# Adding expert rows into the residual by accumulating transfers instead of loads and vector additions

## The chip, the cores and the metric

The kernel runs on one core of a Trainium2 chip. The core has five engines with an instruction queue each: PE (matrix products), DVE (vector), ACT (scalar), POOL (GpSimd) and SP (sync, which here only issues transfers), and 16 DMA engines that all queues share. The metric is the device time of one execution in microseconds. Before the change the median of three runs is 1189.38 us (1186.39 to 1190.62).

## The reference

One transformer block on x of shape [1, 512, 1024], all in fp32: three attention-like branches, a merge, a first residual with layer norm, then a hierarchical mixture of experts (the router picks one of 4 groups and 2 of 8 experts in it, so each of 512 tokens goes to 2 of 32 experts), a second residual and a layer norm. Only the end concerns this change:

```python
    y = jnp.zeros((T, D), h.dtype).at[tok_s].add(w_s[:, None].astype(h.dtype) * ybuf[dest])
...
        y = _hier_moe(x, w_router_group[l], b_router_group[l], w_router_expert[l], b_router_expert[l], w_exp_gate[l], w_exp_up[l], w_exp_down[l])
        x = _layer_norm(DN_ALPHA * x + y, ln2_g[l], ln2_b[l])
```

A token's output is DN_ALPHA (2 to the power 1/4) times its row of x, plus the weighted rows of its two experts, normalized.

## The kernel before, in words

The first 880 us compute the branches, the merge, the first layer norm and the router. The residual x1 stays in SBUF as four chunks c of 128 tokens by 1024. A copy of it goes to DRAM (x1d), from which tokens are gathered for the experts.

The experts' stage walks over 16 pairs of experts, p = 0 to 15. Each pair has 64 rows for either expert. Its 12 weight tiles of 512 KB (tiles j = 0 to 3 gate and up, j = 4 and 5 down) come from DRAM through SP's queue into a ring of 33 buffers (`expert_raw`, load at L114), 96 MB in all. Per pair: `gather` brings the rows (for pairs 0 and 1 by one-hot products with x1 on PE, L767; later by an indirect transfer and transposes, L778), `gate_up` makes 16 matmuls (L789), ACT and DVE make the gated product `esg` (L193, L194, L1006), PE transposes it (L1010), ACT copies it to `ehT` (L1011), and 8 matmuls with the down weights give the rows (L1023). The profile shows each fp32 matmul of these as two records.

What becomes of the rows depends on the pair. For pairs 0 to 13 (PDR = 14) ACT and DVE scale them and POOL scatters them into the DRAM buffer yd (L1037): row k * 512 + t is the k-th expert's row of token t. After the scatter of pair 13 the program reads yd back in eight loads of 512 KB on SP's queue (L1046, into buffers of the ring) and adds them to x1 on DVE (L1048 for k = 0, with the factor ALPHA; L1050 for k = 1). Pairs 14 and 15 do not pass through DRAM: their rows `yp` stay in SBUF as a high and a low part (L1033, L1034), and one-hot products `ohs` put them in place (`add_up`, L982).

The end: for chunk c and half n an accumulator in PSUM gets the matmul identity times x1 (L1062), two one-hot products with pair 14's rows, two with pair 15's; the layer norm reads it (L631 and on) and SP stores the result.

The order of instructions on each engine is chosen by a scheduler when the program is built, from dependences and its own costs; every engine then takes its own instructions strictly in that order, and an instruction that waits holds up all that stand behind it on its engine. The waits on transfers are by semaphores: DMAHW for those of SP, DMASW for those of POOL, eight of each in turn.

Of the kernel before, what the change touches and what calls it, by code (L numbers as in the profile page):

```python
# [16 lines left out]
OP = mybir.AluOpType  # L17
# [5 lines left out]
ALPHA = 2.0 ** 0.25  # L23
# [13 lines left out]
def build(tc, ins, out, dbg=None):  # L37
    nc = tc.nc
# [4 lines left out]
    def T(pool, shape, dt=F32, tag=None, **kw):  # L43
        cnt[0] += 1
        tag = tag or f"u{cnt[0]}"
        return pool.tile(list(shape), dt, name=f"{tag}_{cnt[0]}", tag=tag, **kw)

    def dump(name, ap):
        if name in dbg:
            nc.sync.dma_start(dbg[name], ap)  # L50
# [19 lines left out]
    V, S, TE, G = nc.vector, nc.scalar, nc.tensor, nc.gpsimd  # L70
# [4 lines left out]
    def bank(tag, w=512, dt=F32):  # L75
        t = T(ps, [128, 512], dt, tag=tag)
        return t[:, :w] if w != 512 else t
# [10 lines left out]
    yd = T(mdram, [1024, 1024], tag="yd")  # L88
# [102 lines left out]
    def silu2(t, src):  # L191

        S.activation(t, src, AF.Tanh, scale=0.5)  # L193
        V.scalar_tensor_tensor(t, t, 1.0, src, op0=OP.add, op1=OP.mult)  # L194
# [73 lines left out]
    with cpool:  # L268
        for h in range(4):
# [13 lines left out]
            for c in range(4):  # L283
# [6 lines left out]
                p = T(tp, [128, 256], tag="cp")  # L290
# [262 lines left out]
    x1 = T(sp, [128, 4, 1024], tag="x1")  # L553
# [49 lines left out]
    for k in range(8):  # L603
        S.mul(mh[:, k, :], merged[:, k, :], 0.5)
        V.scalar_tensor_tensor(ml[:, k, :], merged[:, k, :], 0.5, mh[:, k, :].bitcast(F32),
                               op0=OP.mult, op1=OP.subtract)
    p1a.close()

    rp = es.enter_context(tc.tile_pool(name="rawb", bufs=NRAW))
# [5 lines left out]
    def expert_raw(n):  # L615

        while len(raws) < min(n, 192):
            m = len(raws)
            e, j = m // 12 * 2 + m % 2, m % 12 // 2
            pool, tag = ring[m % len(ring)]  # L620
            raws[e, j] = load(ins["wexp"][e, j], pool=pool, tag=tag)
# [100 lines left out]
    for k in range(8):  # L722
        raw = wo_raw[k]
        w0 = T(wp, [128, 1024], F32R, tag="wh", bufs=3)
        split(w0[:, :512], w0[:, 512:], raw[:, :512])
        t = T(wp, [128, 1024], F32R, tag="wl", bufs=3) if k < 3 else T(rp, [128, 1024], F32R, tag="raw")
# [23 lines left out]
    def fetch(p):  # L750
        if PEG <= p < 16:
            G.indirect_dma_start(out=xgs[p % AHEAD], out_offset=None, in_=x1d[:, :],
                                 in_offset=bass.IndirectOffsetOnAxis(ap=gidx[:, p:p + 1], axis=0),
                                 bounds_check=511, oob_is_err=False)

    def gather(p):

        xs = T(mp, [128, 8, 128], tag="xs")
        pts = []
        if p < PEG:  # L760
            oh_ = oh0 if p == 0 else T(mp, [128, 4, 128], tag="ohg", bufs=1)
            pts = [bank("o" if p == 0 else "tr") for _ in range(2)]
            for c in range(4):
                if p > 0:
                    picked(c, p, oh_)
                for k in range(8):
                    TE.matmul(pts[k // 4][:, k % 4 * 128:(k % 4 + 1) * 128], x1[:, c, k * 128:(k + 1) * 128],  # L767
                              oh_[:, c, :], start=c == 0 and k % 4 == 0, stop=c == 3 and k % 4 == 3)
        else:
            xg = xgs[p % AHEAD]  # L770
        for j in range(2):
            if p < PEG:
                pt = pts[j]
            else:
                pt = bank("tr")
                for k in range(4):
                    kk = j * 4 + k
                    TE.transpose(pt[:, k * 128:(k + 1) * 128], xg[:, kk * 128:(kk + 1) * 128], ident)  # L778
            (S.copy if j == 0 else V.tensor_copy)(xs[:, j * 4:(j + 1) * 4, :].rearrange("p k r -> p (k r)"), pt)
        return xs  # L780

    def gate_up(p, xs):

        acc = bank("pj")
        for j in range(4):
            for k in range(2):
                for q in range(2):
                    rows_ = slice(q * 64, (q + 1) * 64)
                    TE.matmul(acc[rows_, :], xs[:, j * 2 + k, rows_], raws[2 * p + q, j][:, k * 512:(k + 1) * 512],  # L789
                              start=j == 0 and k == 0, stop=j == 3 and k == 1)  # L790
        return acc
# [200 lines left out]
    for p in range(16):  # L992
        expert_raw(12 * p + 12 + len(ring))
        gu = gate_up(p, xs)
        if p == 0:
            part = Parts(T(mp, [128, 2048], tag="yp"))
            tables(part)
            overflow_tables(part)
            for j in range(1, AHEAD + 1):
                fetch(j)  # L1000
        if p < 15:
            xs = gather(p + 1)
            fetch(p + 1 + AHEAD)
        sg = T(mp, [128, 256], tag="esg")
        silu2(sg, gu[:, :256])
        V.tensor_tensor(sg, sg, gu[:, 256:], op=OP.mult)  # L1006
        hT = T(mp, [128, 256], tag="ehT")
        pt = bank("tr", 256)
        for k in range(2):
            TE.transpose(pt[:, k * 128:(k + 1) * 128], sg[:, k * 128:(k + 1) * 128], ident)  # L1010
        S.mul(hT, pt, 0.5)  # L1011
        if p < PDR:
            y = T(mp, [128, 2048], tag="yp")
        else:
            yp = T(mp, [128, 2, 1024], F32R, tag="yp")
            ohs = T(mp, [128, 512], F32R, tag="ohs")
            V.tensor_scalar(ohs, i512, tok[:, p:p + 1], None, op0=OP.is_equal)
        for n in range(2):
            acc = bank("o")
            for k in range(2):  # L1020
                for q in range(2):
                    rows_ = slice(q * 64, (q + 1) * 64)
                    TE.matmul(acc[rows_, :], hT[:, k * 128 + q * 64:k * 128 + (q + 1) * 64],  # L1023
                              raws[2 * p + q, 4 + k][:, n * 512:(n + 1) * 512],
                              start=k == 0, stop=k == 1)
            ns = slice(n * 512, (n + 1) * 512)
            if p < PDR:
                if n == 0:
                    S.mul(y[:, ns], acc, wsl[:, p:p + 1])
                else:  # L1030
                    V.tensor_scalar(y[:, ns], acc, wsl[:, p:p + 1], None, op0=OP.mult)  # L1031
            else:
                S.mul(yp[:, 0, ns], acc, wsl[:, p:p + 1])  # L1033
                V.scalar_tensor_tensor(yp[:, 1, ns], acc, wsl[:, p:p + 1], yp[:, 0, ns].bitcast(F32),  # L1034
                                       op0=OP.mult, op1=OP.subtract)
        if p < PDR:
            G.indirect_dma_start(out=yd[:, :], out_offset=bass.IndirectOffsetOnAxis(ap=yidx[:, p:p + 1], axis=0),  # L1037
                                 in_=y[:, 0:1024], in_offset=None, bounds_check=1023, oob_is_err=False)
        else:
            group.append((ohs, yp))  # L1040
        if p == PDR - 1:

            for c in range(4):
                for k in range(2):
                    t = T(rp, [128, 1024], tag="raw")
                    nc.sync.dma_start(t, yd[k * 512 + c * 128:k * 512 + (c + 1) * 128, :])  # L1046
                    if k == 0:
                        V.scalar_tensor_tensor(x1[:, c, :], x1[:, c, :], ALPHA, t, op0=OP.mult, op1=OP.add)  # L1048
                    else:
                        V.tensor_tensor(x1[:, c, :], x1[:, c, :], t, op=OP.add)  # L1050
    dump("gidx", gidx)


# [140 lines left out]
```

## Time and profile before

| | |
|---|---|
| median of three runs | 1189.38 us |
| profiled execution, its own time | 1191.01 us |
| its span, first to last instruction | 1189.1 us |
| mean granted TensorE clock | 0.985 |
| PE, DVE, ACT, POOL busy | 93%, 42%, 37%, 7% |
| SP's transfers (q1) | 183.92 MB, 45.6% of 16 engines' span |
| POOL's transfers (q0) | 15.87 MB, 4.1% |

The shares are means over stages with different limits. From about 950 us to 1145 us the 16 DMA engines are full and PE waits for weights between matmuls; before that PE is nearly always busy. The chain of waits follows what ended last back from the end; a matmul's place in it gives its line. A time of a transfer "to landing" runs from its issue to its semaphore.

### The profile page before, as it was taken

Reading aid. Unit: us, or ns where it says so; the run is one execution under the profiler, and the core shown is the slowest. Engines: PE = TensorE matmul, PEld = TensorE weight load, DVE = VectorE, ACT = ScalarE, POOL = GpSimd, SP = SyncE. Lnnn points to the kernel's source line nnn. Section 1 sums busy time; section 2 is a strip of 40 time slices with the busy share of each in tenths; the row PEclk is TensorE's granted clock in tenths of the full one; section 3 lists DMA queues with packets and bytes.
Section 4 is the critical chain, followed back from the end, with each engine's and each line's share of the span. In section 5 each row is a group of like instructions: output and inputs, shape, how many; then the busy total and the mean of one; then the engine's idle time right before and its main releaser. Section 6 shows DMA issues by size and latency. Waiting matters only on the chain.

```text
span 1189.1 us, 17191 instructions
## 1 busy us (share of the span) xinstructions
PE 1111.0 (93%) x6830; PEld 779.2 (66%) x6830; DVE 504.1 (42%) x998; ACT 442.9 (37%) x762; POOL 84.7 (7%) x104
## 2 busy tenths in 40 slices
PE   6999999999999999999999999999989988888872
PEld 4788677777777887887887877888774333223231
DVE  4544387776676323323224223336574111111145
ACT  6965467665655433233233333225011111101112
POOL 1000130000000000000000000000323111110003
PEclk9999999999999999999999999999999999999986
DMA  8633241222222632322331333335659999999961
GB/s 295 217 94 88 91 130 54 64 81 64 80 63 80 185 105 62 93 89 66 98 97 49 93 91 130 121 100 214 262 195 240 314 408 405 402 403 399 410 254 71
DMA packets 69650, 200.91 MB, mean 169 GB/s; under 512 B 16719, under 2 KB 18843, under 8 KB 69568
## 3 DMA queue, kind: packets, MB, share of 16 engines
q1 hardware_dynamic: 62640, 183.92, 45.6%
q0 software_dynamic: 6928, 15.87, 4.1%
q8 instruction: 55, 0.90, 0.3%
q14 instruction: 27, 0.22, 0.1%
HBM read 191.23 MB, written 17.81 MB: 176 GB/s over the span
## 4 chain that ended last, share of the span: by engine, by line
PE 76%; DMA 13%; ACT 4%; DVE 3%; issue 2%; SPq 0%; ACTq 0%; POOL 0%; DVEq 0%; POOLq 0%
PE pj L131 49%; DMA raw<-in_wexp_dram 11%; PE pj L789 5%; PE tr L217 3%; PE o L1023 3%; PE pj L718 2%; PE o L718 2%; DMA raw<-in_w_in_dram 1%; PE sc L357 1%; PE sc L511 1%; DMA wh<-in_wexp_dram 1%; PE o L533 1%; ACT bvt L338 1%; PE o L299 1%; PE o L530 1%
## 5 line engine op out<-in xcount | busy, mean ns | idle before, releaser
L84 DVE TENSOR_TENSOR wl<-raw,wh 128x1024 fp32r<-128x1024 f32 (+1 forms) x129 | 148.1, 1149 | 268.3 <-PE pj L131 179.1
L83 ACT CAST wh<-raw 128x1024 fp32r<-128x1024 f32 (+1 forms) x137 | 132.3, 967 | 247.9 <-PE pj L131 237.5
L131 PE MATMUL pj<-xh,wh 128*128 128x512 f32 x760 | 204.5, 401 | 5.1 <-ACT wh L83 5.1
L131 PE MATMUL pj<-xl,wh 128*128 128x512 f32 x760 | 199.8, 397 | 0.0
L131 PE MATMUL pj<-xh,wl 128*128 128x512 f32 x760 | 194.1, 394 | 0.0
L131 PEld LDWEIGHTS pj<-xh,wl 128*128 128x128 f32 x760 | 141.8, 188 | 32.5 <-issue 2.1
L131 PEld LDWEIGHTS pj<-xh,wh 128*128 128x128 f32 x760 | 139.8, 189 | 35.1 <-ACT wh L83 6.4
L131 PEld LDWEIGHTS pj<-xl,wh 128*128 128x128 f32 x760 | 140.7, 188 | 29.7 <-issue 0.9
L789 PE MATMUL pj<-raw,xs 128*64 128x512 f32 x432 | 125.2, 605 | 13.0 <-DMA raw<-in_wexp_dram 12.1
L789 PEld LDWEIGHTS pj<-raw,xs 128*64 128x64 f32 x432 | 36.0, 137 | 82.3 <-issue 49.3
L193 ACT ACTIVATE esg<-pj 128x256 f32<-128x256 f32 x16 | 6.1, 384 | 134.8 <-PE pj L789 134.8
L194 DVE SCALAR_TENSOR_TENSOR esg<-esg,pj 128x256 f32<-128x256 f32 x16 | 6.7, 421 | 116.8 <-ACT esg L193 116.8
L1023 PE MATMUL o<-raw,ehT 128*64 128x512 f32 x204 | 52.5, 604 | 1.2 <-ACT ehT L1011 0.5
L1031 DVE TENSOR_SCALAR yp<-o,wsl 128x512 f32<-128x512 f32 x14 | 10.5, 750 | 69.9 <-PE o L1023 69.8
L388 ACT ACTIVATE bx<-bx 128x512 f32<-128x512 f32 x48 | 30.4, 633 | 19.3 <-DVE bx L387 18.7
L1023 PEld LDWEIGHTS o<-raw,ehT 128*64 128x64 f32 x204 | 16.6, 140 | 28.6 <-issue 24.0
L131 PE MATMUL pj<-oh,wh 128*128 128x512 f32 x128 | 34.9, 400 | 0.0
L131 PE MATMUL pj<-oh,wl 128*128 128x512 f32 x128 | 34.3, 395 | 0.0
L131 PE MATMUL pj<-ol,wh 128*128 128x512 f32 x128 | 33.2, 391 | 0.0
L209 DVE SCALAR_TENSOR_TENSOR sg<-sg,pj 128x512 f32<-128x512 f32 x16 | 11.0, 686 | 40.2 <-PE pj L131 40.2
L131 PEld LDWEIGHTS pj<-ol,wh 128*128 128x128 f32 x128 | 24.0, 188 | 5.3
L131 PEld LDWEIGHTS pj<-oh,wl 128*128 128x128 f32 x128 | 23.9, 188 | 5.2
(377 smaller groups left out, 1448.1 us busy)
## 6 DMA issues: line engine op xcount, KB each, us to landing
raw<-in_wexp_dram SPq DMA_DIRECT2D x159, 512.0 KB, 11.1
raw<-in_w_in_dram SPq DMA_DIRECT2D x95, 512.0 KB, 3.6
wh<-in_wexp_dram SPq DMA_DIRECT2D x18, 512.0 KB, 11.3
wl<-in_wexp_dram SPq DMA_DIRECT2D x15, 512.0 KB, 11.3
yd<-merged SPq DMA_DIRECT2D x8, 512.0 KB, 6.3
raw<-in_w_kv_dram SPq DMA_DIRECT2D x8, 512.0 KB, 3.7
raw<-in_w_bb_dram SPq DMA_DIRECT2D x8, 512.0 KB, 3.6
raw<-in_w_out_dram SPq DMA_DIRECT2D x8, 512.0 KB, 3.8
```

Of the source, the lines that this page charges most:

```text
L83: S.copy(h, src)
L84: (eng or V).tensor_tensor(l, src, h.bitcast(F32), op=OP.subtract)
L131: TE.matmul(acc, wt[:, k * 128:(k + 1) * 128], m[:, k, :], start=n == 0, stop=n == 3 * kt - 1)
L217: TE.transpose(pt[:, j * 128:(j + 1) * 128], src[:, j * 128:(j + 1) * 128], ident)
L299: TE.matmul(o[:, cs], v[:, js], pT[:, js], start=j == 0, stop=j == 1)
L338: S.copy(nat(vT), cls(acc))
L357: TE.matmul(sc[g * 32:(g + 1) * 32, j * w:(j + 1) * w].rearrange("p (a t) -> p a t", t=32), keys[:, gs], queries[:, :, gs], start=True, st ...
L388: S.activation(X, X, AF.Exp)
L511: TE.matmul(s1[g * 32:(g + 1) * 32, :], qs[0][:, c * 128 + g * 32:c * 128 + (g + 1) * 32], ks[0][:, lows[g] * 128:lows[g] * 128 + 256], st ...
L718: TE.matmul(acc, m[:, k, cs], w[:, j * 512:(j + 1) * 512], start=k == 0 and n == 0, stop=k == 7 and n == 2)
L789: TE.matmul(acc[rows_, :], xs[:, j * 2 + k, rows_], raws[2 * p + q, j][:, k * 512:(k + 1) * 512], start=j == 0 and k == 0, stop=j == 3 and ...
L1023: TE.matmul(acc[rows_, :], hT[:, k * 128 + q * 64:k * 128 + (q + 1) * 64], raws[2 * p + q, 4 + k][:, n * 512:(n + 1) * 512], start=k == 0, ...
```

## The change

The eight loads into buffers and the eight additions on DVE go. POOL issues eight transfers from yd that add into x1 in SBUF (`accum_op`), first the four chunks of k = 0, then the four of k = 1. The factor ALPHA, which was part of the addition for k = 0, becomes four multiplications of x1 on ACT, written in the program at pairs 4 to 7. The rest of the program is as before; lines after L1001 shift by two, and those after the block by minus three, so L1010, L1023 and L1062 are L1012, L1025 and L1059 in the changed kernel.

```diff
@@ -1001,6 +1001,8 @@
         if p < 15:
             xs = gather(p + 1)
             fetch(p + 1 + AHEAD)
+        if 4 <= p < 8:
+            S.mul(x1[:, p - 4, :], x1[:, p - 4, :], ALPHA)
         sg = T(mp, [128, 256], tag="esg")
@@ -1040,14 +1042,9 @@
             group.append((ohs, yp))
         if p == PDR - 1:
 
-            for c in range(4):
-                for k in range(2):
-                    t = T(rp, [128, 1024], tag="raw")
-                    nc.sync.dma_start(t, yd[k * 512 + c * 128:k * 512 + (c + 1) * 128, :])
-                    if k == 0:
-                        V.scalar_tensor_tensor(x1[:, c, :], x1[:, c, :], ALPHA, t, op0=OP.mult, op1=OP.add)
-                    else:
-                        V.tensor_tensor(x1[:, c, :], x1[:, c, :], t, op=OP.add)
+            for k in range(2):
+                for c in range(4):
+                    G.dma_start(x1[:, c, :], yd[k * 512 + c * 128:k * 512 + (c + 1) * 128, :], accum_op=OP.add)
```

The scheduler moves more than these lines. In the rows below `x` is x1, `raw`, `wh` and `wl` are weight buffers, `ident` is the identity, and the words in brackets are the semaphores that the instruction waits for.

On POOL, behind the scatter of pair 13 (L1039), stand the eight accumulating transfers:

```order
L1039 DMA yd_69<-yp_8982,yidx_6596 1024x1024 [waits DMASW6_49,DMASW7_49,DVE_49,Activation_49]
L1047 DMA x_1119_6592<-yd_69 128x1024 [waits DMASW7_49]
L1047 DMA x_1119_6592<-yd_69 128x1024 [waits DMASW1_49]
L1047 DMA x_1119_6592<-yd_69 128x1024
L1047 DMA x_1119_6592<-yd_69 128x1024 [waits DMASW3_49]
L1047 DMA x_1119_6592<-yd_69 128x1024 [waits DMASW0_49]
L1047 DMA x_1119_6592<-yd_69 128x1024 [waits DMASW1_49]
L1047 DMA x_1119_6592<-yd_69 128x1024 [waits DMASW2_49]
L1047 DMA x_1119_6592<-yd_69 128x1024 [waits DMASW3_49]
```

The first waits for the scatter (DMASW7) and takes DMASW0; the fifth to eighth (k = 1) each wait for the one of the same chunk (DMASW0 to 3) and take DMASW4 to 7. Before, POOL's next instruction after this scatter was an elementwise product of the last layer norm.

On PE before, at the end of pair 14's gate and up products (L789), the transposes and the down products (L1023) of the same pair follow, and the first product with x1 (L1062) stands behind all of pair 15:

```order
L789 MATMUL pj_9018<-raw_8790,xs_8956 64x512
L789 MATMUL pj_9018<-raw_8792,xs_8956 64x512
L1010 MATMUL tr_9053<-ident_61,esg_9048 128x128 [waits DVE_49,Activation_49]
L1010 MATMUL tr_9053<-ident_61,esg_9048 128x128
L1023 MATMUL o_9060<-raw_8794,ehT_9052 64x512 [waits DMAHW5_49,Activation_49]
...
L1023 MATMUL o_9110<-raw_8937,ehT_9095 64x512
L1062 MATMUL sc_9121<-x_1119_6592,ident_61 128x512 [waits DVE_49]
```

On PE in the changed kernel, the same place at the end of pair 14's L789:

```order
L789 MATMUL pj_9006<-raw_8794,xs_8960 64x512
L789 MATMUL pj_9006<-raw_8796,xs_8960 64x512
L1059 MATMUL sc_9109<-x_1119_6592,ident_61 128x512 [waits DMASW4_49]
L1012 MATMUL tr_9041<-ident_61,esg_9036 128x128 [waits DVE_49,Activation_49]
L1012 MATMUL tr_9041<-ident_61,esg_9036 128x128
L1059 MATMUL sc_9110<-x_1119_6592,ident_61 128x512
L1025 MATMUL o_9048<-raw_8798,ehT_9040 64x512 [waits DMAHW5_49,Activation_49]
```

The product with chunk 0 has moved ahead of pair 14's transposes and down products, and waits for the fifth accumulating transfer (chunk 0, k = 1). A little further on PE, at the start of pair 15's L789 (accumulator pj_9062):

```order
L982 MATMUL sc_9109<-yp_9045,ohs_9046 128x512 [waits Activation_49]
L789 MATMUL pj_9062<-raw_8864,xs_9023 64x512 [waits DMAHW1_49]
L982 MATMUL sc_9109<-yp_9045,ohs_9046 128x512 [waits DVE_49]
L982 MATMUL sc_9110<-yp_9045,ohs_9046 128x512 [waits Activation_49]
L982 MATMUL sc_9110<-yp_9045,ohs_9046 128x512 [waits DVE_49]
L1059 MATMUL pj_9113<-x_1119_6592,ident_61 128x512 [waits DMASW6_49,PE_49]
L789 MATMUL pj_9062<-raw_8866,xs_9023 64x512 [waits DMAHW2_49]
```

Fifteen of pair 15's sixteen L789 now stand behind chunk 0's one-hot products with pair 14's rows and behind a product with chunk 2, which waits for the seventh accumulating transfer. Between pair 15's transposes and its down products stands one product with chunk 1; behind the down products come pair 14's one-hot products and the products with x1 that are left of chunks 1 and 2, then pair 15's one-hot products and chunk 3 last, as before.

On ACT the four multiplications by ALPHA do not stand at pairs 4 to 7 but at pairs 0 and 1: the first ahead of the copy of pair 0's gathered rows (L779), two ahead of that copy for pair 1, and the fourth between it and pair 0's `ehT` copy (L1013). On SP the eight loads of yd are gone, and the loads of the last layer norm's gain and bias follow the last weights directly.

## Rows read from the trace of the kernel before

**Rows 1.** Two windows: length, engines' busy us (records), PEclk, DMA, GB/s.

```profile
950.00:965.00 15.00, 14.72 (x68) 5.14 (x66) 2.19 (x4) 2.04 (x4) 3.03 (x3) 1.00 1.03 409
1120.00:1130.00 10.00, 7.87 (x33) 3.04 (x34) 1.87 (x4) 2.04 (x4) 0.00 (x0) 1.00 1.03 410
```

**Rows 2.** The chain of waits at the end: start us, us, what.

```profile
1120.12 1.95 PE pj L789 x6
...
1125.28 10.18 DMA wh<-in_wexp_dram
...
1135.50 1.95 PE pj L789 x6
...
1139.85 5.44 PE o L1023 x16
...
1145.33 0.70 ACT yp L1033
...
1146.05 0.61 DVE yp L1034
...
1148.51 1.22 DVE x L1050
...
1149.77 1.46 PE sc L1062 x2
...
1154.34 0.86 PE tr L1062 x2
1155.20 0.47 PE tr L982 x2
...
1159.62 0.93 PE sc L982 x4
...
1164.57 0.94 PE o L982 x4
```

**Rows 3.** The timeline of DVE: start us, us, what.

```profile
1146.71 1.21 DVE L1048 SCALAR_TENSOR_TENSOR x<-x,raw 128x1024 f32<-128x1024 f32 x1
```

**Rows 4.** The timeline of SP's queue, and the landing of its last weights.

```profile
1129.13 1.60 SPq L114 DMA_DIRECT2D raw<-in_wexp_dram  x2
1131.70 9.24 SPq L1046 DMA_DIRECT2D raw<-yd  x8
...
DMA to landing us min/median/max: 10.2/10.2/10.2
```

**Rows 5.** DMA queues from 1120 to 1141 us: packets, MB, share of 16 engines.

```profile
q1 hardware_dynamic: 2357, 8.59, 102.6%
```

**Rows 6.** DMA queues from 1066.5 to 1069.5 us, where POOL's transfers meet the weights.

```profile
q1 hardware_dynamic: 199, 0.73, 63.4%
q0 software_dynamic: 195, 0.45, 38.6%
```

**Rows 7.** Pair 13's scatter: issue, landing; DMA queues from 1113.7 to 1116.4.

```profile
1113.74 0.97 POOL L1037 DMA_INDIRECT yd<-yp,yidx  x1 [15.27 <-DVE xs L779]
...
DMA to landing us min/median/max: 6.6/6.6/6.6
...
q1 hardware_dynamic: 306, 1.11, 102.7%
```

**Rows 8.** PE: pair 14's L1023, an unhindered L789, a window at half clock.

```profile
1124.47 3.70 PE L1023 MATMUL o<-raw,ehT 128*64 128x512 f32 x16 [0.53 <-ACT ehT L1011]
...
922.30 6.00 PE pj L789 x26
...
1141.00:1142.00 1.00, 1.00 (x4) 0.29 (x3) 0.00 (x0) 0.00 (x0) 0.00 (x0) 0.50 1.02 406
```

**Rows 9.** ACT: an operation on 128x1024 (from the page), and two copies at pair 0.

```profile
L83 ACT CAST wh<-raw 128x1024 fp32r<-128x1024 f32 (+1 forms) x137 | 132.3, 967 | 247.9 <-PE pj L131 237.5
...
901.41 0.59 ACT L779 COPY xs<-tr 128x512 f32<-128x512 f32 x1 [4.50 <-PE tr L767]
902.53 0.38 ACT L1011 ACTIVATE ehT<-tr 128x256 f32<-128x256 f32 x1 [0.53 <-PE tr L1010]
```

## The prediction, made before the changed kernel ran

> **What bounds the kernel now.** I read the windows of busy time first, since the shares of the page are means over stages. From 950 us on the 16 DMA engines are full (share 1.03, 409 GB/s) while PE is still nearly full; by 1120 us PE is busy 7.87 of 10 us and the engines remain at 410 GB/s [rows 1]. So the experts' stage ends when the last weights have come, and whatever is put ahead of them on the DMA engines moves the end.
>
> The chain of waits then shows the end piece by piece. Pair 14's L789 ends at 1122.07, PE takes its L1023 at 1124.47, and a weight tile that lands at 1135.46 releases the last of pair 15's L789. Pair 15's L1023 runs from 1139.85 to 1145.29, ACT and DVE turn it into `yp`, DVE finishes chunk 0 of x1 at 1149.73, and PE starts L1062 at 1149.77 and is done at 1165.51 [rows 2]. Behind this comes the layer norm with its stores, which the change leaves alone.
>
> The last two weight loads are issued in the 1.60 us from 1129.13, the second at about 1130.4, and land 10.2 us later; the last weight is there at 1140.6. Only then do the eight loads of yd, issued from 1131.70 in the same queue, get the engines [rows 4]. From 1120 to 1141 us that queue alone moved 8.59 MB and filled the engines [rows 5], at 409 GB/s, so 512 KB take 1.28 us of all 16 engines.
>
> **What the change removes.** Eight DVE operations of about 1.2 us (9.7 us) [rows 3], of which the first two stand on the path: between the end of pair 15's L1023 and PE's first L1062 lie 4.5 us. In the new order the products with chunks 0 to 2 are spread ahead of and among pair 15's work. If x1 were ready at once and the weights came as before, what is left of PE's work behind pair 15's down products (L1025) would be three L982 groups of 0.47 and two L1059 of 0.86, together 3.1 us, which also cover ACT's and DVE's work on `yp`, and then what ran from 1159.62 to 1165.51, 5.9 us [rows 2]. PE would end 9.0 us after L1025 instead of 20.2 us after: a gain of 11.2 us. That is all there is to gain.
>
> **What it adds on the DMA engines.** The first accumulating transfer waits for the scatter of pair 13, which was issued at 1113.74 and landed 6.6 us later, at 1120.3. That scatter's own packets were not yet among those moved up to 1116.4, where SP's queue is alone, so a transfer of POOL needs about 2.7 us before it moves anything [rows 7]. I take 1123.0 for the first accumulating packet. At that time about 13 weight loads are still to come (17.6 us to 1140.6 at 1.28 us). So the new transfers do not run behind the weights, as the loads of yd did, but among them.
>
> What one costs the trace does not show. Below, it costs what a plain transfer of 512 KB does, 1.28 us. Above, it costs as much as reading yd, reading x1 and writing x1 as three plain transfers, 3.84 us. I take two, 2.57 us: the sum needs 512 KB of yd and 512 KB of x1 read, and a plain transfer already reads and writes at once in its 1.28 us. The Trainium skill, Collectives: The Full Stack, in The bandwidth ceiling, says that an addition inside a transfer is slow not for the adder but because two sources must be read on one ring, which halves its rate. No run before the change shows that; by it the price would be the middle one, and it speaks against the change.
>
> How the two queues share the engines rests on a row: with two of POOL's transfers under way from 1066.5 to 1069.5 us, its queue had 38.6% of the engines' time and the weights 63.4% [rows 6], less than half since the backlog had gaps. I take packets in turn: one of 4 KB of weights, then one accumulating packet at double price. The Trainium skill, DMA: Bandwidth & Descriptors, Queues, rings and completion order, also says that each engine goes round its queues by whole packets; the row agrees, and does not tell whether both reads of an addition count as one.
>
> **The sum.** While both queues are full, one accumulating transfer and one weight load take 2.57 + 1.28 = 3.85 us. The fifth, for which PE's first L1059 waits, ends at 1123.0 + 5 x 3.85 = 1142.3; the seventh at 1150.0; the eighth at 1153.8. All eight are through before the last weight, which they delay by 8 x 2.57 = 20.6 us, to 1161.2.
>
> By PE's order: PE stands still from 1122.07 to 1142.3. Then two L1059 (0.86 each) and L1012 (0.42), 2.1 us; half clock after the pause, which stretched 3.70 us of L1023 to 5.44 at pair 15, where a window shows 0.50 [rows 2, 8], 1.7; L1025 3.7; ACT 0.70 and DVE 0.61 on `yp`, 1.3; the last L982 and chunk 2's L1059, 1.3: 10.1 us. Pair 15's L789 at 0.23 a record [rows 8], 30 records, 6.9, and L982 0.47; from there to L1025 the 2.4 us of today (1137.45 to 1139.85); L1025 3.7; then 9.0. Together 32.6 us: PE ends at 1174.9.
>
> By the weights: today L1023 ends 4.7 us after the last weight; 1161.2 + 4.7 + 9.0 = 1174.9. Both ways meet, against 1165.5 today: 9.4 us later.
>
> **Edits at the margin.** The four multiplications on ACT are priced by the nearest row of that shape, 0.97 us [rows 9]. The first three fit ahead of copies that wait for PE's gather; the fourth stands between pair 1's copy at 901.41 and pair 0's `ehT` at 902.53, and can begin only when the gather ends, at about 902.1, so that copy comes up to 0.6 us late. PE is full there; the order gives it two more L789 to do meanwhile, and I charge 0.3 us (0 to 1). The eight issues on POOL hold up nothing: what stands behind them is wanted after 1160 us. The ring of 33 buffers does not run dry while PE stands: the last weight, the 192nd, needs only the buffer of the 159th, a tile of pair 13. The gain and bias of the last norm come earlier, with no one waiting.
>
> Total: 9.4 + 0.3 = 9.7 us later. The profiled execution took 1191.01 us around a span of 1189.1, 1.6 us above the median; its sum is 1200.7, and from the median 1189.4 I forecast 1199.1 us.
>
> **The rivals.**
>
> One read's price: 1.28 us, packets in turn. The fifth ends at 1123.0 + 5 x 2.57 = 1135.8, PE ends 32.6 later at 1168.4, the last weight comes at 1150.9 and would allow 1164.6. 2.9 us and 0.3 later: 1192.6. For it speaks that plain transfers already read and write at once; against it, that the sum has two sources.
>
> A dearer share: either three transfers' price, or two reads that each take their turn against a weight packet. Both put the fifth at 1123.0 + 5 x 5.13 = 1148.7 and the seventh at 1158.9. From the seventh PE has 0.86 + 7.4 + 2.4 + 3.7 + 9.0 = 23.4 us left: 1182.3, or 1206.5 in all. At three transfers' price the last weight is at 1171.4 and PE ends at 1185.1: 1209.3.
>
> Slower still: the chain k = 1 behind k = 0 leaves POOL's queue empty between transfers, or adding is slower than reading. Then PE stands until late with pair 15's work behind it: over 1211.
>
> The other side, not slower: POOL's queue takes the engines whole when it has work, at one read's price. The fifth ends at 1129.4, PE by its order at 1162.0, and the last weight at 1150.9 decides, 1164.6: 0.9 us less, 1188.8 with ACT's charge. It decides from the point where five transfers and the weights between them take under 9.9 us, 2.0 each. Against it stands the share of 38.6% [rows 6]. Only a price below a plain load's makes the kernel faster: each 1.28 us less for the eight is worth as much.
>
> **How the numbers follow.** Two reads, in turn: 0.42, 1199.1. Dearer share: 0.25, 1206.5 to 1209.3. Slower still: 0.08. One read: 0.13, 1192.6. Not slower: 0.12, 1188.8, of which 0.04 with a lower price yet. The range from 1190 to 1211 leaves out the last and the slowest. No change is within 0.3%, 3.6 us. One read's 3.2 us lies at that edge, so I split it: slower 0.42 + 0.25 + 0.08 + 0.06 = 0.81, same 0.07 + 0.08 = 0.15, faster 0.04.
>
> **What the changed profile would show.** If I am right: no DVE operation on x1 after 1146 us; the first L1047 issued at about 1120; PE idle from 1122 to some 1142 us, released by a transfer into x1; POOL's queue with two thirds of the engines from 1123 to 1154 if both reads are counted, or half; weight loads there landing 3.9 us apart rather than 1.3; the last weight at about 1161; from the end of pair 15's L1025 to the end of PE's work 9 us rather than 20. Wrong would be a fifth transfer that lands before 1130, or weights that still end near 1141, for then the DMA engines were not the limit; or PE waiting for x1 beyond 1160.

## The result, and the profile after

The changed kernel takes 1203.61 us (median; 1203.01 to 1207.35) where the kernel before, on the same chip, takes 1187.89 us (1185.76 to 1190.62): a ratio of 1.0141, interval 1.0116 to 1.0166, some 14 to 20 us slower (the medians differ by 15.7). In a second comparison it was 1.0147 [1.0131, 1.0162]. The profiled execution of after took 1203.36 us around a span of 1201.6.

Profiled executions differ in what comes ahead of the change: the scatter of pair 13 was issued at 1113.74 us in before [rows 7], at 1112.48 and 1110.50 in two executions of after, and at 1108 to 1112 in the experiments. So I measure from the issue of that scatter to the span's end, since everything that the change moves on the path lies there, but for ACT's multiplications (e2): 75.4 us before, 89.1 after (13.7 more), 89.5 in after's second profile. This measure too varies between profiles: e2, whose median time is that of before, has 73.8, so 1 or 2 us between single profiles decide nothing.

The chain of waits of after, from pair 13's scatter on (start us, us, what), answers to [rows 2]:

```profile
1112.48 6.70 DMA yd<-yp,yidx
1119.48 8.46 DMA x<-yd
1128.22 15.00 DMA x<-yd
1143.27 2.07 PE sc L1059 x2
...
1147.13 3.63 PE o L1025 x16
...
1156.50 5.31 PE pj L789 x22
...
1164.47 3.63 PE o L1025 x16
...
1176.35 0.94 PE o L982 x4
```

Where the path of before ran over weights, `yp` and VectorE's additions, it now runs for 30 us over DMA transfers alone: the scatter, the first accumulating transfer, and from its landing another 15.0 us to the landing of the fifth. Only then does PE go on, and it ends at 1177.29 where it ended at 1165.51.

The issues on POOL (start us, us, line, what, count, and the idle time before with what ended it):

```profile
1119.48 3.69 POOL L1047 DMA_DIRECT2D x<-yd  x4 [6.02 <-DMA yd<-yp,yidx]
1128.22 0.86 POOL L1047 DMA_DIRECT2D x<-yd  x1 [5.06 <-DMA x<-yd]
1132.07 0.86 POOL L1047 DMA_DIRECT2D x<-yd  x1 [2.99 <-DMA x<-yd]
1135.88 0.86 POOL L1047 DMA_DIRECT2D x<-yd  x1 [2.94 <-DMA x<-yd]
1139.71 0.86 POOL L1047 DMA_DIRECT2D x<-yd  x1 [2.97 <-DMA x<-yd]
```

The transfers of k = 1 each wait for the landing of the one of k = 0 on the same rows, so the last four issues are a clock for the landings of the first four: one in 3.81 to 3.85 us. In [rows 5] a plain load of that size took 1.28.

The two queues from 1127 to 1140 us (packets, MB, share of 16 engines), to set beside [rows 6]:

```profile
q0 software_dynamic: 494, 1.79, 68.8%
q1 hardware_dynamic: 496, 1.80, 36.8%
```

As many packets of accumulation (q0) as of weights (q1), but nearly twice the engines' time for them. The total is 276 GB/s where [rows 1] has 410, with the engines just as full.

PE's side: its row behind the pause, and the windows of the pause and what follows (length, engines' busy us, PEclk, DMA, GB/s):

```profile
1143.27 2.07 PE L1059 MATMUL sc<-x,ident 128*128 128x512 f32 x2 [22.50 <-DMA x<-yd]
...
1122.00:1143.00 21.00, 0.00 (x0) 0.00 (x0) 0.10 (x1) 0.00 (x0) 4.61 (x6) 0.60 1.06 280
1143.00:1146.00 3.00, 2.73 (x5) 1.49 (x6) 0.00 (x0) 0.13 (x1) 0.00 (x0) 0.50 1.06 276
```

PE issues no product for 22.5 us, and starts again at 0.50 of its clock (1.2 GHz). SP's last two weight loads, issued within 1.60 us in [rows 4], now take 4.18, since SP waits ahead of each for an earlier weight load to land, and these land more slowly:

```profile
1134.92 4.18 SPq L114 DMA_DIRECT2D raw<-in_wexp_dram  x2
```

### The profile page after: what moved, and what is told of

Read it like the earlier page. It is cut to its first block, busy times and chain, and to the rows that moved or that the text cites. A ratio compares the mean times of both kernels' runs of the same rounds, so it can differ in the third digit from the quotient of the medians.

```text
span 1201.6 us, 17185 instructions
## 1 busy us (share of the span) xinstructions
PE 1110.5 (92%) x6830; PEld 778.7 (65%) x6830; DVE 495.3 (41%) x990; ACT 446.8 (37%) x766; POOL 91.8 (8%) x112
## 4 chain that ended last, share of the span: by engine, by line
PE 76%; DMA 14%; ACT 3%; DVE 3%; issue 2%; SPq 0%; ACTq 0%; POOL 0%; DVEq 0%; POOLq 0%
PE pj L131 50%; DMA raw<-in_wexp_dram 7%; PE pj L789 5%; PE tr L217 3%; PE o L1025 3%; DMA wl<-in_wexp_dram 2%; DMA x<-yd 2%; DMA wh<-in_wexp_dram 2%; PE pj L718 2%; PE o L718 2%; PE sc L357 1%; PE sc L511 1%; PE o L533 1%; ACT bvt L338 1%; PE o L299 1%
## 5 line engine op out<-in xcount | busy, mean ns | idle before, releaser
L789 PE MATMUL pj<-raw,xs 128*64 128x512 f32 x432 | 125.0, 605 | 11.2 <-DMA raw<-in_wexp_dram 10.3
L789 PEld LDWEIGHTS pj<-raw,xs 128*64 128x64 f32 x432 | 35.1, 137 | 80.9 <-issue 50.7
L1025 PE MATMUL o<-raw,ehT 128*64 128x512 f32 x204 | 51.7, 600 | 0.7
L1025 PEld LDWEIGHTS o<-raw,ehT 128*64 128x64 f32 x204 | 16.5, 138 | 27.9 <-issue 22.5
```

## The experiments

Runs of one group shared a chip and its runs of before: e1, e2, e3 and e6 (before there 1186.29 us); e4, e5, e7 and after again (1186.75); e9 and e10 (1186.38). "From the scatter" is the time from pair 13's scatter to the span's end, of the profiled execution.

| run | what it is | median us | ratio to before | from the scatter us |
|---|---|---|---|---|
| before | | 1186.3 to 1187.9 | 1 | 75.4 |
| after, again | | 1203.37 | 1.0147 [1.0131, 1.0162] | 89.5 |
| e1 | after with plain loads, the addition left out | 1196.15 | 1.0076 [1.0049, 1.0103] | 82.9 |
| e2 | before with ALPHA on ACT | 1186.19 | 0.9999 [0.9984, 1.0013] | 73.8 |
| e3 | after, x1's product last | 1198.18 | 1.0089 [1.0059, 1.0118] | 88.0 |
| e6 | after with four of eight transfers, the rows of k = 1 left out | 1195.16 | 1.0070 [1.0047, 1.0092] | 81.6 |
| e4 | before, x1's product last | 1184.15 | 0.9975 [0.9961, 0.9989] | 73.3 |
| e5 | after, transfers behind the weights | 1196.96 | 1.0087 [1.0072, 1.0102] | 84.5 |
| e7 | after without the eight transfers, the rows of pairs 0 to 13 left out | 1177.43 | 0.9916 [0.9899, 0.9933] | 65.5 |
| e9 | e5 and e3 together | 1189.47 | 1.0029 [1.0018, 1.0039] | 77.4 |
| e10 | e4 with ALPHA on ACT and half the additions on POOL | 1183.71 | 0.9979 [0.9968, 0.9990] | 70.4 |

**The changed kernel once more.**

> The changed kernel unchanged, on the chip of the others, so that each stands against it in the same rounds. By the first comparison 1.2 to 1.7 per cent above before, 14 to 20 us; from the issue of pair 13's scatter to the span's end 89 us, against 75 in before.

It came out so: 1.0147, and 89.5 us from the scatter.

**Plain loads in place of accumulating ones (e1).**

```diff
-  G.dma_start(x1[:, c, :], yd[...], accum_op=OP.add)
+  G.dma_start(x1[:, c, :], yd[...])
```

> The eight transfers stay on POOL's queue at the same places but no longer accumulate: plain loads of yd that overwrite x1, so the addition is left out. Theory (an accumulating transfer costs two reads, a plain one a single read, packets in turn with the weights): POOL's issues of the fifth to eighth transfer come 2.6 us apart rather than 3.8, the fifth lands at about 1136.5 rather than 1143.2, PE starts its first product with x1 6.5 us earlier, and the time is about 1197. Rival (POOL's queue or the waits between the transfers set the pace, not the second read): the spacing stays 3.8 us and the time stays within 2 us of 1203.6.

The last four issues on POOL, PE's row behind the pause, and the two queues from 1122 to 1132 us:

```profile
1124.46 0.53 POOL L1047 DMA_DIRECT2D x<-yd  x1 [5.15 <-DMA x<-yd]
1127.02 0.53 POOL L1047 DMA_DIRECT2D x<-yd  x1 [2.03 <-DMA x<-yd]
1129.58 0.53 POOL L1047 DMA_DIRECT2D x<-yd  x1 [2.03 <-DMA x<-yd]
1132.14 0.53 POOL L1047 DMA_DIRECT2D x<-yd  x1 [2.03 <-DMA x<-yd]
...
1134.47 2.08 PE L1059 MATMUL sc<-x,ident 128*128 128x512 f32 x2 [15.96 <-DMA x<-yd]
...
q1 hardware_dynamic: 565, 2.06, 51.4%
q0 software_dynamic: 561, 2.04, 51.2%
```

Same places, same bytes written: 2.56 us apart instead of 3.83, equal shares of the engines, 410 GB/s. 2.56 is two plain prices of 1.28, one of the transfer and one of the weight load beside it; 3.83 is three. So an accumulating transfer costs two, the middle of the prediction's three prices. PE's first L1059 comes 24.3 us after the scatter instead of 30.8, and the time from the scatter is 6.2 to 6.6 us shorter, as the theory of two reads had it. But the plain loads too make the kernel 0.8% slower than before, of 1.5% with the addition: about half of the loss is not in the addition.

**ALPHA on ACT in the kernel before (e2).**

```diff
+  if 4 <= p < 8:
+      S.mul(x1[:, p - 4, :], x1[:, p - 4, :], ALPHA)
...
-  V.scalar_tensor_tensor(x1[:, c, :], x1[:, c, :], ALPHA, t, op0=OP.mult, op1=OP.add)
+  V.tensor_tensor(x1[:, c, :], x1[:, c, :], t, op=OP.add)
```

> The kernel before with one part of the change: ALPHA multiplied on ACT at the places of the change, and the additions for k = 0 on DVE without the factor. Theory: the fourth multiplication delays pair 0's ehT copy by 0.5 us and PE has other products meanwhile: 0 to 0.6 us, time within 1 us of before. Rival (the multiplications upset the start of the experts' stage and account for a part of the loss): 2 us or more later than before.

0.9999, at most 2 us either way: no cost of ACT's part of the change is seen. PE's down products of pairs 14 and 15 in e2, to set beside [rows 8] and [rows 2]:

```profile
1119.49 5.38 PE o L1025 x16
...
1134.87 3.75 PE o L1025 x16
```

Here the half clock (window 1120 to 1125: 0.69 of full speed in the mean) falls on pair 14 and is made good while PE would wait for weights: pair 15's L789 end 23.7 us after the scatter in both. In before it falls on pair 15 (5.44 us, pair 14's 3.70), behind the weights. These 1.7 us are what e2 is shorter from the scatter, 73.8 against 75.4: the profile of before is a long one, and against e2 the changed kernel is 15.3 to 15.7 us longer, not 13.7.

**PE's order and the weights, taken apart (e3, e5, e9).** In after two things could hold the end: PE's order, in which the product with x1 opens every accumulator and so stands ahead of pair 15's work, and the transfers' place among the weights, which come late then. e3 removes the first:

```diff
-  TE.matmul(accs[c][n], ident, x1[:, c, ...], start=True, stop=False)
-  add_up(accs[c][n], c, n, group[:1], False, False)
+  add_up(accs[c][n], c, n, group[:1], True, False)
...
-  add_up(accs[c][n], c, n, group[1:], False, True)
+  add_up(accs[c][n], c, n, group[1:], False, False)
+  TE.matmul(accs[c][n], ident, x1[:, c, ...], start=False, stop=True)
```

> The changed kernel, but each output accumulator takes the rows of pairs 14 and 15 first and the product with x1 last, so PE has no product with x1 ahead of pair 15's work. The transfers are as in the change. Theory (PE's place for the product with x1 turns late chunks into a stop of the whole engine): PE goes on at 1122 with pair 14, paced by weights that share the engines until about 1153, the last weight lands near 1155 to 1157, PE ends about 1169 to 1171 rather than 1177.3, time 1196 to 1198. Rival (the delayed weights alone set the end, PE's order costs nothing): the end of PE stays near 1177 and the time within 2 us of 1203.6.

PE's timeline in e3, where it works on pair 15 without waiting for x1:

```profile
1135.90 3.49 PE L789 MATMUL pj<-raw,xs 128*64 128x512 f32 x6 [2.72 <-DMA raw<-in_wexp_dram]
1139.74 1.07 PE L789 MATMUL pj<-raw,xs 128*64 128x512 f32 x2 [0.36 <-DMA raw<-in_wexp_dram]
1143.54 3.32 PE L789 MATMUL pj<-raw,xs 128*64 128x512 f32 x6 [2.72 <-DMA raw<-in_wexp_dram]
1147.39 1.07 PE L789 MATMUL pj<-raw,xs 128*64 128x512 f32 x2 [0.53 <-DMA raw<-in_wexp_dram]
1151.19 1.12 PE L789 MATMUL pj<-wh,xs 128*64 128x512 f32 x1 [2.72 <-DMA wh<-in_wexp_dram]
...
1160.83 1.94 PE L1025 MATMUL o<-raw,ehT 128*64 128x512 f32 x8
...
1174.32 1.02 PE L1091 MATMUL o<-x,ident 128*128 128x512 f32 x2
```

PE starts again at every weight that lands, and these come 3.8 us apart. Pair 15's L1025 is over 53.7 us after the scatter (1162.8); in after, behind the long pause, 55.6 us (1168.1). Behind it e3 has more left to do, since the products with x1 now come last: PE needs 12.6 us to its end (1175.3), where after needs 9.6 by the same timeline. Of the order alone 6 to 8 us were expected, and in the profile the time from the scatter fell by only 1.1 to 1.5. By the times it was no miss: the median of 1198.18 us is at the edge of the 1196 to 1198 expected, and the ratio, 1.0089 against 1.0147, is 6 to 7 us below after's. The five runs lie between 1193.99 and 1201.41 us, and there is one profile. What the order alone is worth, 1 us or 7, stays open.

e5 removes the second: a tiny operation on POOL reads the last weight, and its result, zero, is added to one column of x1 ahead of the transfers:

```diff
+  expert_raw(192)
+  zw = T(mp, [128, 1], tag="zw", bufs=1)
+  G.tensor_scalar(zw, raws[31, 5][:, 0:1], 0.0, None, op0=OP.mult)
+  for c in range(4):
+      G.tensor_tensor(x1[:, c, 0:1], x1[:, c, 0:1], zw, op=OP.add)
```

> The changed kernel with its accumulating transfers held back until the last expert weight has landed (a tiny GpSimd operation reads that weight into x1's first column, times zero). With nothing else on the DMA engines a transfer of 512 KB shows its own price: by two reads about 2.6 us from one to the next, where it was 3.85 beside the weights; if the spacing is set by the issue or by a fixed price of an accumulating transfer, it stays at 3.8. The weights are not delayed: the last is issued and lands about as in before (about 1140), pair 15's products run at once, and the end hangs on the transfers alone: fifth landing about 1157, eighth about 1164.5, TensorE's end about 1168, the time about 2 to 3 us above before. Rival (price fixed at 3.85): eighth landing about 1174, end about 1178, the time 12 to 13 us above before.

Its issues on POOL, its queue from 1143 to 1153 us, and the first and the last of PE's rows behind its pause:

```profile
1143.53 0.86 POOL L1052 DMA_DIRECT2D x<-yd  x1 [1.77 <-DMA x<-yd]
1146.21 0.86 POOL L1052 DMA_DIRECT2D x<-yd  x1 [1.81 <-DMA x<-yd]
1148.82 0.86 POOL L1052 DMA_DIRECT2D x<-yd  x1 [1.75 <-DMA x<-yd]
...
q0 software_dynamic: 566, 2.08, 105.6%
...
1153.63 2.04 PE L1064 MATMUL sc<-x,ident 128*128 128x512 f32 x2 [13.46 <-DMA x<-yd]
...
1169.15 1.97 PE L982 MATMUL o<-yp,ohs 128*128 128x512 f32 x6
```

The price came out as expected: 2.5 to 2.7 us each with nothing beside them, the engines full at 208 GB/s. The Trainium skill, Collectives: The Full Stack, in The bandwidth ceiling, says that adding halves a ring's rate because two sources are read; 208 against 410 GB/s agrees. The landings were right too: the fifth 43.1 us after the scatter (expected 43.3). The time was not: +10.3 us where 2 to 3 were expected. The expectation let PE be done with all but the last product; in fact the fifth landing releases a row of L1064 and L982 products for all four chunks, which take 17.5 us, half clock at first. e9 repairs that, with both edits:

> The changed kernel with both corrections at once: the accumulating transfers held behind the last weight (as in the run before, where they came 2.6 us apart, the fifth landing 43.1 us and the eighth 50.9 us after the issue of pair 13's scatter), and the product of x1 last in every accumulator, so that TensorE has its other work done before they land. Then only the eighth landing and its two products remain: TensorE's end about 53 to 54 us after that scatter (before 52.2, the run before 60.8), span's end about 76.5 to 78 after it, the time 1 to 3 us above before. If so the miss of the run before was TensorE's order and not the transfers. Rival: TensorE at half clock after its pause, or the tail behind four products that come 2.6 us apart, costs more: over 5 us above before.

PE's timeline in e9:

```profile
1145.48 2.03 PE L982 MATMUL o<-yp,ohs 128*128 128x512 f32 x8
1152.74 3.75 PE L1096 MATMUL sc<-x,ident 128*128 128x512 f32 x4 [5.23 <-DMA x<-yd]
...
1160.18 1.95 PE L1096 MATMUL o<-x,ident 128*128 128x512 f32 x4
```

All L982 stand ahead of the pause, and behind it are four groups of x1's product. PE ends 53.7 us after the scatter (expected 53 to 54), the span 77.4 (76.5 to 78), and the kernel is 0.3% above before. The four corners by the ratio: 1.0147 as changed, 1.0089 with the order alone mended, 1.0087 with the weights alone undisturbed, 1.0029 with both. Each hindrance is worth some 0.6%, and the two add up. From the scatter, one profile each, they are 89.1 to 89.5, 88.0, 84.5 and 77.4 us, where each alone gives less. By either measure more than half of the loss is left when one alone is removed, so neither is the cause by itself. Even so the accumulating version is not the equal of loads and additions: with PE's order mended in both, e9 (1.0029) is 0.5% above e4 (0.9975, below).

**Half of the transfers (e6).**

```diff
-  for k in range(2):
+  for k in range(1):
```

> Only the four accumulating transfers of k = 0; those of k = 1 are left out (half of the rows of pairs 0 to 13 are missing from the sum). PE's first product with x1 then waits for the first transfer, not the fifth. Theory (PE's stop lasts to the transfer of chunk 0 that it waits for, then some 34 us of PE's work follow): PE goes on at about 1128, and the weights, late by 4 x 2.57 = 10 us, become the limit: PE ends at about 1164, time 1189 to 1191, so nearly all of the loss goes with half of the transfers. Rival (each transfer costs the same share of the loss): half the loss stays, about 1196.

A miss: +0.7%, or about half of the loss, which is the rival's number. PE's timeline shows that it comes about in another way:

```profile
1111.22 4.50 PE L789 MATMUL pj<-raw,xs 128*64 128x512 f32 x18
1127.79 2.07 PE L1059 MATMUL sc<-x,ident 128*128 128x512 f32 x2 [12.06 <-DMA x<-yd]
1129.79 3.54 PE L789 MATMUL pj<-raw,xs 128*64 128x512 f32 x6
```

With fewer transfers the order puts x1's product still earlier, now ahead of pair 14's last 14 L789. PE waits 12.06 us for the first transfer and has more work left behind it than after. So the run doesn't measure half the price; it shows that the scheduler's order follows the edit.

**No transfers at all (e7).**

```diff
-  for k in range(2):
+  for k in range(0):
```

> The changed kernel without its eight transfers: the rows of pairs 0 to 13 that went through DRAM are left out, ScalarE's multiplications and the scatters stay. The gain term alone: x1 is ready early, nothing slows the weights, TensorE's end about 9 us after the last down projections where it was 20.2: about 11.2 us below before (TensorE's end about 1154.3 by the clock of before). With the changed kernel's +14 to +18 this makes the cost of the transfers some 25 to 29 us. Rival: the front part or the tail takes the gain back, less than 5 us below before.

0.9916, 10.0 us less than before (8 to 12 by the interval), and 9.9 from the scatter (8.3 against e2): the prediction's gain term of 11.2, alone. Against after in the same rounds the eight transfers cost 24 us (from the scatter) to 27 (by the ratios), and the rest of the change gives 10 back.

**The same gain without the change (e4, e10).** e4 is the kernel before with e3's edit.

> The kernel before with one thing moved: the product of the residual x1 with the identity closes each accumulator's group in place of opening it, so TensorE no longer waits for VectorE's last additions before pair 15's down projections. If the 11.2 us of waiting that the prediction counted as gain lie in that wait alone, they are to be had here without any accumulating transfer, but for the products themselves (2 us) and the wait for the last addition that is left at the very end (x1 ready at 1149.8 in the trace of before, TensorE's end 1165.5): TensorE's end at about 1159.6 to 1160 by the clock of that trace, 4 to 5.5 us below before. Rival: the wait hides another (the plain loads land late enough, or the products at the end cost as much): within 2 us of before.

Faster by 0.25% (1.3 to 4.6 us). PE's last product ended 49.5 us after the scatter instead of 52.2, and 1.7 of this are the half clock in before's profile (e2 has 50.5); expected was 4 us or more. VectorE's timeline and PE's last row:

```profile
1144.88 1.22 DVE L1048 SCALAR_TENSOR_TENSOR x<-x,raw 128x1024 f32<-128x1024 f32 x1
...
1155.78 0.68 DVE L631 BATCH_NORM_STATS2 lnst<-tr 128x6 f32<-128x512 f32 x1
1156.38 1.20 DVE L1050 TENSOR_TENSOR x<-x,raw 128x1024 f32<-128x1024 f32 x1
...
1157.64 1.99 PE L1094 MATMUL o<-x,ident 128*128 128x512 f32 x4 [0.94 <-DVE x L1050]
```

Now PE waits for the additions, and these, which took 10.2 us in a row before, are spread over 12.7 with the layer norm's statistics between them. e10 gives the additions of the first two chunks to POOL; it also has ALPHA on ACT, as in e2, so that an addition stands for either k:

```diff
-  V.tensor_tensor(x1[:, c, :], x1[:, c, :], t, op=OP.add)
+  (G if c < 2 else V).tensor_tensor(x1[:, c, :], x1[:, c, :], t, op=OP.add)
```

> Not the change but what it was for: the kernel before with x1's product last (the run that was 0.25 per cent faster), ALPHA on ScalarE, and the additions of the first two of x1's four row blocks on GpSimd, which is idle there, so that they needn't stand behind the last yp operation on VectorE (1144.2 in that run, though the first load had landed at about 1138). VectorE's four additions end about 5 to 6 us earlier (some 1152 by that trace, where the last ended at 1157.6), GpSimd's four at 2.6 to 3.4 us each (two of its 128x512 additions) end at 1149 to 1152. TensorE's end about 1153.5 to 1155 where it was 1159.6: 5 to 6 us below that run, about 8 us below before, which is near the run without any transfers (10 us). Rival: the two engines slow each other down, or the row blocks that TensorE wants first come last: no better than that run.

Its POOL and VectorE:

```profile
1140.07 9.60 POOL L1049 TENSOR_TENSOR x<-x,raw 128x1024 f32<-128x1024 f32 x4 [27.16 <-DMA raw<-yd]
...
1148.54 0.70 DVE L631 BATCH_NORM_STATS2 lnst<-sc 128x6 f32<-128x512 f32 x1 [2.78 <-PE sc L1093]
...
1156.10 1.60 DVE L1049 TENSOR_TENSOR x<-x,raw 128x1024 f32<-128x1024 f32 x1
```

POOL did its four in 9.60 us, 2.4 each where 2.6 to 3.4 were expected. VectorE gained little: its order puts chunk 0's statistics ahead of the other additions, so it idles 2.78 us for PE and ends its last addition 45.8 us after the scatter, against 47.4 in e4, and PE ends at 49.3 against 49.5. The ratio is e4's (0.9979 against 0.9975): the rival. In the one profile the time from the scatter is 2.9 us shorter (70.4 against 73.3), nearly all of it in the layer norm behind PE's end, which the times don't confirm.

## Why the prediction was right, and by how much each step missed

The mechanism and the sign were right, and the measured time lies in the range; the size was forecast as +9.7 us and came out as 13.7 from the scatter and 16.8 by the ratio, so the sum was too small by three to four tenths. By the time alone, 1203.61 us lies between the forecast (1199.1) and the rival of a dearer share (1206.5 to 1209.3), nearer to the rival; what decides for the forecast's mechanism is the spacing of 3.83 us.

| step | predicted | measured |
|---|---|---|
| gain if x1 were ready at once | 11.2 us | 10.0 (e7) |
| ACT's multiplications | 0.3 | not seen (e2, at most 2) |
| accumulating transfer beside a weight load | 3.85 | 3.81 to 3.85 (after) |
| its own price | 2.57 (two reads) | 2.5 to 2.7 alone (e5); 2.5 to 3.2 (e9); one plain price more than e1 |
| POOL's queue while both are full | two thirds | 68.8% |
| first landing, from the scatter | 13.1 | 15.5 |
| fifth landing, from the scatter | 28.6 | 30.7 |
| PE from there to its end | 32.6 | 34.1 |
| from L1025's end to PE's end (by the chain) | 9.0 | 9.2 |
| span's end behind PE's end | as before, 23.6 | 24.3 |

**The price and the sharing** were chosen between ends far apart and hit. The row on which the sharing rested, [rows 6], was enough for packets in turn, and the new one (494 against 496 packets) settles what it left open: both reads of an accumulating packet count as one turn. That rules out the rival of 5.13 us a transfer. The Trainium skill, DMA: Bandwidth & Descriptors, in Queues, rings and completion order, says as much of whole packets; the trace agrees in that both queues move equal numbers of them, and does not show how many go in one turn.

**The term that was too small** is the way to the first landing. I let the first packet move 2.7 us behind the scatter's landing and the first transfer take 3.85 from there, together 13.1 us after the scatter's issue; it took 15.5. POOL's queue in the 4.0 us from the first issue, and from there to the first landing at 1127.94 (packets, MB, share of 16 engines):

```profile
q0 software_dynamic: 18, 0.07, 12.1%
...
q0 software_dynamic: 161, 0.59, 66.7%
```

The first packet was on time, 2.5 to 3.0 us behind the issue (none had moved by 1122.0, four by 1122.5). But the queue did not come to its two thirds at once, and at the first landing 0.66 MB had moved, where one transfer has 0.52. At the second row's pace the first 0.52 MB were through some 7.4 us behind the issue, an estimate from these rows; the sum had 6.2, and the landing came at 8.5. So about half of the miss is the slow start and half a landing that comes later than the transfer's own amount of bytes. The sum had neither. On empty engines the first transfer landed 5.2 us (e5) and 6.2 us (e9) behind its issue; why the start is slow the rows don't say. From there four more at 3.83 give the fifth landing within 0.1 us, 2.1 us later than forecast. Behind it PE took 1.5 us longer, most of it in pair 15's L789: 32 records in 8.2 us, where the sum had 30 in 6.9. With 0.7 us in the layer norm's tail, which was not forecast, and ACT's 0.3 not paid, these are the 4.0 us between 9.7 and 13.7. Another 1.6 us were not in the change at all: the sum was set against a profile of before with half clock on the path (e2).

**Both ways meet** held in the profiles: by the weights alone (e3) pair 15's L1025 ends 53.7 us after the scatter, by the order (after) 55.6; predicted was 52.2 for both. So which of the two the chain of after names, the transfers, is decided by 2 us. If both ways always met so closely, mending one of them should bring little; the times, by which e3 and e5 each bring 0.6% and e9 the sum of both, don't bear that out, and with one profile of each it is not shown.

**What stays open.** The ratio says 16.8 us (14 to 20), the rows from the scatter on 13.7. Of the 3 us between them 1.6 lie behind the scatter, in the long profile of before: against e2 the rows say 15.3 to 15.7, within the ratio's interval. The rest may lie ahead of the scatter, whose issue moves between 1108.5 and 1113.7 us from one profiled execution to the next; whether the change also costs something there, one profile each can't tell. The landing of the last weight in after can't be read exactly, since nobody waits for it. The engines' share falls from 1.04 (1150 to 1155 us) to 0.40 (1155 to 1160) and 0.02 behind that, with two loads of the last norm still behind the weights, so it came before 1160, 47.5 us after the scatter, where 47.5 was forecast.

## What to carry to other kernels

A transfer that accumulates saves vector operations, but it moves two sources: where the DMA engines are the bound, price it as twice the bytes, and add what it delays in the queue that it shares. A plain load queued behind the weights in one queue cost the weights nothing here: the last one landed 26.9 us after the scatter in before, and 26.7 in e5, where no load of yd stands in that queue. The same load issued early on another queue shared the engines with them half and half (e1). And look where the consumer stands in its engine's order: moving a product to the end of its accumulation (e4) gave 0.25% without a single transfer changed, and only with that and the place behind the weights did the accumulating version come within 0.3% of before.

## What the runs showed of the hardware

- Accumulating into SBUF halves the rate: 208 GB/s at a share of 1.06 of the engines (e5), 410 for plain packets at 1.03 (e1).
- The issue of an accumulating transfer on POOL takes 0.86 us against 0.53 for a plain one of the same shape (after, e1).
- After 22.5 us without a product PE's granted clock was 0.50 (1.2 GHz) in the window from 1143 to 1146 us, and two L1059 took 2.07 us where two at full clock, at 1152.95, took 1.02; in e9 four took 3.75 against 1.95.
- Additions on 128x1024 take GpSimd 2.4 us each (four in 9.60, e10), VectorE 1.2 [rows 3].
